# Gated projection with its last two column chunks tile by tile, its split weights in two sets, and a new buffer layout for the second layer's experts

## Chip, cores and metric

One core of one Trainium2 chip runs the whole kernel, one launch. The metric is the device time of one execution in microseconds. The kernel was timed three times; profiled times come from one further execution.

## What is computed

The reference is a trunk of two layers on 1024 positions of width 1024, in float32. Each layer is a token mixer and a mixture of experts, each with its own normalisation. Cut to what the change touches:

```python
def s5_mixer(h, ...):                    # the mixer of layer 1
    ...                                  # state space, y: 1024 x 1024
    y = jax.nn.gelu(y)
    z = y @ w_glu                        # 1024 x 2048: the gated projection
    return z[..., :D] * jax.nn.sigmoid(z[..., D:])

def hierarchical_moe(h, ...):            # behind both mixers
    g_prob = softmax(xt @ w_group + b_group)          # 4 groups, the best one
    e_logits = xt @ w_expert + b_expert               # its 8 experts, the best two
    ...                                               # lists of rows for 32 experts
    hid = silu(xblk @ w_gate[e]) * (xblk @ w_up[e])   # each expert on its rows
    return hid @ w_down[e]

for layer in range(2):
    x = x + g1 * mix(rms_norm(x) * (1 + sc1) + sh1)
    h = rms_norm(x) * (1 + sc2) + sh2
    x = x + g2 * hierarchical_moe(h, ...)
```

## The kernel before

The 1024 positions are eight tiles of 128. A float32 product is made of three products of halves: each operand is split into a high part (a rounding copy) and a low part (a subtraction), and high-high, high-low and low-high are summed in PSUM.

**The gated projection** is the second half of `mixer_b`. Its stationary inputs are `yh[i]` and `yl[i]`, the two parts of the activated tile i. Its weights are taken in four chunks c of 256 columns of each half (value and gate). The loop at L1754 runs over 32 units (chunk, tile): chunk by chunk, and in a chunk tile by tile. A unit is 24 matmuls of 512 columns (L1770), 6 for each quarter q of the contraction. ScalarE's tanh (L1777), a combination on VectorE (L1778) and two operations for the residual update of `x2` (L1780, L1781) follow; the last two are on VectorE for chunk 3 and on GpSimd for the others. `load(c)` brings a chunk of the weights (2 MB) into two buffers of the 16-KB ring; `split(c, q)` makes a quarter's parts `gh` on ScalarE (L1745) and `gl` on VectorE, or GpSimd for half of chunk 0 (L1746). There is one set of `gh` and `gl` of four quarters; the next chunk's are split in the last unit of a chunk. The order of TensorE's work is as written; the other engines follow a scheduler's order.

**The router** (`moe_front`) works beside the projection, in layer 0 beside the attention's output product (L624). Of a unit that is finished, `squares` transposes the columns of the residual (`pt`, L701) and sums their squares on ScalarE, `logits` multiplies them with the router's weights (`lg`, L709) and adds to `lga` (L712). When a tile has all its columns, `scale` finishes the reciprocal root of the mean square with thirteen short operations (L720 to L118) and applies it and the bias to the logits (L723, L724); `rows_in` (L730) and `rows_out` (L736) make the tile's normalised row `hr` and GpSimd stores it to `hrow` in memory (L737). In layer 1, tiles 0 to 5 do so in their groups of three, and two `hr` buffers are in use; in layer 0 there is one, and each tile is scaled by itself. `route` runs for the groups of tiles 0 to 2, 3 to 5 and 6 to 7: VectorE chooses group and experts (L760 to L782, the last being `seen`), TensorE makes prefix sums (`lp`, L786, L787), VectorE makes slots (`so`, L808), and TensorE adds the group to the lists (`lst`, L813). `moe_lists` reads the lists (`lit`, `ligi`, L891, L892). GpSimd then gathers rows by index (`xg`, L956). A tile named `f13hr` is that of layer 1, tile 3; `r10`, `r13` and `r16` are the groups that begin with tile 0, 3 and 6 of layer 1, and `r06` is the last of layer 0.

**The experts** (`moe`): 32 per layer. Gate and up weights of an expert (2 MB) lie in a pair, down weights (1 MB) in a ring buffer x. In both layers experts take turns on two pairs of the ring `w` and two pairs of their own. The SP queue issues all weight loads in program order, each when its buffer is free.

## Time and profile before

| | us |
|---|---|
| median of three runs (lowest, highest) | 1853.67 (1853.0, 1856.04) |
| the profiled execution, its own time | 1852.55 |
| its span, first to last instruction | 1850.6 |
| TensorE busy | 1559.9 (84%) |
| VectorE busy | 1255.6 (68%) |
| ScalarE busy | 748.9 (40%) |
| GpSimd busy | 441.7 (24%) |

The mean granted clock of TensorE is 0.922 of full speed (2.4 GHz). The span is 1.95 us shorter than the execution's own time. Busy shares are means over stages of different kinds: the projection stands at 1220 to 1435 us, the experts of layer 1 behind 1481 us, the end of layer 0's mixer at 500 us.

### The profile page before, as it was taken

To read this page: it belongs to the slowest core of one execution; us is meant where nothing else is said; L and a number is where in the kernel's file an instruction comes from. 1 tells how busy PE (TensorE), PEld (TensorE's weight loads), DVE (VectorE), ACT (ScalarE), POOL (GpSimd) and SP (SyncE) were. 2 spreads that over 40 slices of the span, in tenths; PEclk is the share of its full clock that TensorE was granted. 3 is DMA by queue.
4 is the path that set the end of the run, shared out by engine and by line. 5 is a ranking of instruction groups with operands and counts; after the bars stand their busy time and mean duration, and the time that the engine had idled before them with its cause. 6 is when DMAs were issued, how large, how long until landed. Compare 5 with 4: busy or idle time off the path is not lost. (4 is left out here: it accounts for less than half of the span.)

```text
span 1850.6 us, 20822 instructions
## 1 busy us (share of the span) xinstructions
PE 1559.9 (84%) x6935; PEld 1120.2 (61%) x6935; DVE 1255.6 (68%) x2336; ACT 748.9 (40%) x1455; POOL 441.7 (24%) x385
## 2 busy tenths in 40 slices
PE   5799969899769898899799676769998299999990
PEld 2566623387556666566377565658887277777760
DVE  4886679775578987677355799751226767777764
ACT  3211137611155555455311565532221165656540
POOL 1400014520122121111000677432210212222210
PEclk8799989999879999999899788889999599999995
DMA  9656750062469899887453111421111299999947
GB/s 363 216 211 253 293 153 1 22 220 95 164 230 341 328 328 326 324 312 268 152 208 110 32 36 43 135 76 46 47 46 46 106 389 357 364 382 387 369 149 280
DMA packets 124997, 379.85 MB, mean 205 GB/s; under 512 B 44908, under 2 KB 63428, under 8 KB 94168
## 3 DMA queue, kind: packets, MB, share of 16 engines
q1 hardware_dynamic: 94648, 301.89, 45.2%
q0 software_dynamic: 23040, 50.37, 7.4%
q10 hardware_dynamic: 7200, 26.22, 3.8%
q8 instruction: 57, 0.93, 0.2%
q14 instruction: 52, 0.43, 0.1%
HBM read 355.43 MB, written 56.53 MB: 223 GB/s over the span
## 5 line engine op out<-in xcount | busy, mean ns | idle before, releaser
L1770 PE MATMUL gpo<-gh,yh 128*128 128x512 f32 x256 | 107.1, 418 | 9.8 <-ACT gh L1745 9.8
L1770 PE MATMUL gpo<-gl,yh 128*128 128x512 f32 x256 | 101.7, 397 | 1.7 <-POOL gl L1746 1.7
L1770 PE MATMUL gpo<-gh,yl 128*128 128x512 f32 x256 | 101.6, 397 | 0.0
L956 POOL DMA_INDIRECT xg<-hrow,ligi x64 | 83.6, 1307 | 32.1 <-issue 14.9
L1778 DVE SCALAR_TENSOR_TENSOR gth<-gth,gpo 128x256 f32<-128x256 f32 x32 | 13.4, 420 | 110.4 <-ACT gth L1777 110.4
L222 DVE SCALAR_TENSOR_TENSOR acc<-w,cs,acc 128x2048 f32<-128x2048 f32 x35 | 83.6, 2387 | 4.6 <-DMA w<-in_w_ada 4.1
L1770 PEld LDWEIGHTS gpo<-gh,yh 128*128 128x128 f32 x256 | 49.3, 193 | 18.4 <-ACT gh L1745 10.1
L624 PE MATMUL wopo<-woh,a_hi 128*128 128x512 f32 x128 | 55.4, 433 | 1.7 <-ACT woh L598 1.7
L1770 PEld LDWEIGHTS gpo<-gl,yh 128*128 128x128 f32 x256 | 49.3, 192 | 10.6 <-POOL gl L1746 2.2
L1770 PEld LDWEIGHTS gpo<-gh,yl 128*128 128x128 f32 x256 | 48.9, 191 | 10.6
L624 PE MATMUL wopo<-wol,a_hi 128*128 128x512 f32 x128 | 52.6, 411 | 1.9 <-POOL wol L599 1.9
L1678 PE MATMUL bpo<-wih,bhh 128*128 128x512 f32 x128 | 52.3, 408 | 1.8 <-ACT bhh L1668 1.8
L624 PE MATMUL wopo<-woh,a_lo 128*128 128x512 f32 x128 | 52.6, 411 | 0.0
L1678 PE MATMUL bpo<-wil,bhh 128*128 128x512 f32 x128 | 51.3, 401 | 0.0
L1678 PE MATMUL bpo<-wih,bhl 128*128 128x512 f32 x128 | 50.5, 403 | 0.3 <-DVE bhl L1669 0.2
L1780 POOL TENSOR_TENSOR gth<-gth,g 128x256 f32<-128x256 f32 x24 | 17.5, 729 | 110.0 <-DVE gth L1778 110.0
L1680 DVE SCALAR_TENSOR_TENSOR u<-bpo,n_y,shw 128x512 f32<-128x512 f32 x16 | 12.0, 750 | 29.5 <-PE bpo L1678 29.5
L1678 PEld LDWEIGHTS bpo<-wih,bhh 128*128 128x128 f32 x128 | 24.6, 192 | 9.0 <-ACT bhh L1668 3.7
L624 PEld LDWEIGHTS wopo<-woh,a_hi 128*128 128x128 f32 x128 | 25.5, 200 | 7.2 <-ACT woh L598 2.6
L624 PEld LDWEIGHTS wopo<-wol,a_hi 128*128 128x128 f32 x128 | 25.5, 199 | 7.1 <-POOL wol L599 2.3
L1490 POOL TENSOR_TENSOR s0p<-pw_re,bb 128x512 f32<-128x512 f32 x1 | 1.1, 1082 | 118.4 <-DVE n_y L114 118.4
L1678 PEld LDWEIGHTS bpo<-wih,bhl 128*128 128x128 f32 x128 | 24.4, 191 | 7.5 <-DVE bhl L1669 1.8
(2728 smaller groups left out, 4882.6 us busy)
## 6 DMA issues: line engine op xcount, KB each, us to landing
ring<-in_moe_w_down SPq DMA_DIRECT2D x64, 1024.0 KB
w<-in_w_ada SPq DMA_DIRECT2D x48, 1024.0 KB
w<-in_moe_w_gate SPq DMA_DIRECT2D x32, 1024.0 KB
w<-in_moe_w_up SPq DMA_DIRECT2D x32, 1024.0 KB
pair<-in_moe_w_gate SPq DMA_DIRECT2D x32, 1024.0 KB
pair<-in_moe_w_up SPq DMA_DIRECT2D x32, 1024.0 KB
w<-in_ssm_w_glu SPq DMA_DIRECT2D x16, 512.0 KB
w<-in_attn_w_qkv SPq DMA_DIRECT2D x6, 1024.0 KB
```

Source lines behind the costliest of these rows:

```text
L222: eng.scalar_tensor_tensor(acc, w, self.cs[:, j:j + 1], acc, op0=ALU.mult, op1=ALU.add)
L624: T.matmul(po, a[:, kk, j], w[:, j, :], start=(i == 0), stop=(i == 23))
L956: G.indirect_dma_start(out=self.xg, out_offset=None, in_=me.hrow[l], in_offset=bass.IndirectOffsetOnAxis(ap=self.gcol, axis=0), bounds_che ...
L1490: G.tensor_tensor(self.p1, self.power(me.pw_re, 8), self.channel(me.bb1, 8), op=ALU.mult)
L1678: T.matmul(po, a[:, 4 * hf + j, :], w[:, j, :], start=(k == 0), stop=(k == 23))
L1680: V.scalar_tensor_tensor(u[:, 32 * c:32 * c + 32, 7 - i, :], po.rearrange("p (g c) -> p g c", c=16), r, self.shw[:, 512 * c:512 * c + 512] ...
L1770: T.matmul(po, a[:, 2 * q + j, :], w[:, j, :], start=(n == 0), stop=(n == 23))
L1778: V.scalar_tensor_tensor(th, th, 1.0, po[:, 0], op0=ALU.add, op1=ALU.mult)
L1780: E.tensor_tensor(th, th, g1[:, cs], op=ALU.mult)
```

## The change

**Order of the projection.** `unit_order` puts chunks 0 and 1 chunk by chunk, then for each tile chunk 2 and chunk 3 in a row. Units 0 to 15 are as before, units 16 to 31 are (tile 0, chunk 2), (0, 3), (1, 2) and so on. For layer 0, with two column parts, the order stays.

**Weights.** A quarter has its own load of 512 KB into one of two buffers `graw`, and there are two sets of `gh` and `gl`, for even and odd chunks. The quarters of chunk 1 are split in units 1, 3, 5, 7, those of chunk 2 in units 9, 11, 13, 15, and all of chunk 3 in unit 15.

**Residual update.** It is on VectorE for chunks 2 and 3 of tiles 3 to 7 (10 units), else on GpSimd (22).

**Router, both layers.** The chain of the reciprocal root stands ahead of the last addition of logits; scale and bias are one operation. Each tile is scaled and stored by itself, with one `hr` buffer. In `route`, the rows of the last tile are scaled and stored behind the choice of experts, before gates, slots and lists.

**Buffers.** The ring `w` is closed behind the state space. The experts of layer 1 have four pairs p0 to p3 and three x buffers of their own: p0, x0, p1, x1 where `yl` and `yh` of early tiles lie, p2 and x2 where those of the last tiles and `gl` lie, p3 where the router's tiles lie. Their first loads are issued as p0, x0, p1, x1, p2, x2, p3.

```diff
@@ unit_order
+        return sorted(((m, c) for m in range(NT) for c in range(parts)),
+                      key=lambda u: (u[1], u) if u[1] < parts - 2 else (parts, u))
@@ moe_front
-        gain = fp.tile([P, D], F32, name=f"gain2{l}", tag="hr", bufs=1 + l)
+        gain = fp.tile([P, D], F32, name=f"gain2{l}", tag="hr")
...
+            if c == parts - 1:
+                v = fp.tile([P, 1], F32, name=f"v{l}{m}", tag="v")
+                V.tensor_reduce(v, vs[:, m], AX.X, ALU.add)
+                V.tensor_scalar(v, v, 1.0 / D, EPS, op0=ALU.mult, op1=ALU.add)
+                self.rsqrt(fp, v, [P, 1], "n", r)
             if c:
                 V.tensor_tensor(lg_all[:, m], lg_all[:, m], lg[:, :36], op=ALU.add)
...
+            if c == parts - 1:
+                V.scalar_tensor_tensor(lg_all[:, m], lg_all[:, m], r, br, op0=ALU.mult, op1=ALU.add)
...
+            V.tensor_tensor(ex, mc[:, 1], mc[:, 0], op=ALU.subtract)
+            self.last_exp = S.activation(ex, ex, AF.Exp)
+            if m1 == NT:
+                rows_out(NT - 1)
             V.tensor_scalar(sv["eid"][:, ms, :], mi, -1.0, float(NE), op0=ALU.mult, op1=ALU.add)
             V.tensor_reduce(sg, eg, AX.X, ALU.add)
-            V.tensor_tensor(ex, mc[:, 1], mc[:, 0], op=ALU.subtract)
-            self.last_exp = S.activation(ex, ex, AF.Exp)
...
-                if l == 0 or (c == parts - 1 and m >= GROUPS[-2]):
-                    rows_in(m, width * c, width * c + width)
+                if l == 0 or c >= parts - 2:
+                    rows_in(m, width * c if c > parts - 2 else 0, width * c + width)
...
+            if c == parts - 1 and m + 1 < NT:
+                rows_out(m)
@@ moe
+        if l:
+            weights_in(opened("rga"), "p3")
+            weights_in(opened("rgb"), "p0", "p1", "x0", "x1", "p2")
+            weights_in(opened("rgc"), "x2")
+        else:
+            weights_in(opened("rg", side="right"), "x0", "x1", "x2", "p2", "p3")
...
-                w = self.wpair() if e % GU < N1 else pairs[e % GU - N1]
+                w = pairs[e % GU] if l or e % GU >= N1 else self.wpair()
@@ mixer_b
+            src = wrp.tile([P, 2, 512], F32, name=f"graw{c}{q}", tag="graw", bufs=2)
+            w4 = src.rearrange("p a (h n) -> p a h n", h=2)
+            for h in range(2):
+                self.dma(w4[:, :, h], I["ssm_w_glu"][256 * q:256 * q + 256, 1024 * h + 256 * c:1024 * h + 256 * c + 256]
+                         .rearrange("(a p) n -> p a n", p=P))
+            hi = (wp if c % 2 else wrp).tile([P, 2, 512], F32R, name=f"gh{c}{q}", tag=f"gh{q}")
+            lo = wp.tile([P, 2, 512], F32R, name=f"gl{c}{q}", tag=f"gl{c % 2}{q}")
...
-            for k, (c, i) in enumerate((c, i) for c in range(4) for i in range(NT)):
+            for k, (i, c) in enumerate(self.unit_order(4)):
...
-                    if i == NT - 1 and c < 3:
-                        split(c + 1, q)
+                    if q == 3 and c < 2 and i % 2:
+                        split(c + 1, i // 2)
+                    if (i, c) == (NT - 1, 1):
+                        split(3, q)
...
-                E = V if c == 3 else G
+                E = V if c > 1 and i > 2 else G
```

TensorE before, at the end of the projection (`gpo` is its product; `f17` is the last tile's part of the router):

```order
L1770 MATMUL gpo_11177<-gl_10790,yh_9522 128x512
L1770 MATMUL gpo_11177<-gh_10789,yl_9523 128x512
L786 MATMUL r13lp<-oh_9796,after 128x192
L787 MATMUL r13lp<-seen_9797,ones 128x192
L701 MATMUL f173pt<-ident,x_9683 128x128 x2
L709 MATMUL f163lg<-wr_9770,f163ht 128x128 x2
L813 MATMUL lst_9793<-rv_9799,r13so 128x128 x6
L709 MATMUL f173lg<-wr_9770,f173ht 128x128 x2
L786 MATMUL r16lp<-oh_9796,after 128x128
L787 MATMUL r16lp<-seen_9797,ones 128x128
```

TensorE now, in the last unit but one, where the middle group's prefix product stands:

```order
L1771 MATMUL gpo_11292<-gl_10188,yh_9515 128x512
L1771 MATMUL gpo_11292<-gh_10187,yl_9516 128x512
L715 MATMUL f162lg<-wr_9765,f162ht 128x128 x2
L790 MATMUL r13lp<-oh_9791,after 128x192
L791 MATMUL r13lp<-seen_9792,ones 128x192
L1771 MATMUL gpo_11292<-gh_10276,yh_9515 128x512
L1771 MATMUL gpo_11292<-gl_10277,yh_9515 128x512
```

And now behind the last projection matmul:

```order
L1771 MATMUL gpo_11349<-gh_10482,yl_9516 128x512
L707 MATMUL f173pt<-ident,x_9676 128x128 x2
L715 MATMUL f172lg<-wr_9765,f172ht 128x128 x2
L715 MATMUL f173lg<-wr_9765,f173ht 128x128 x2
L790 MATMUL r16lp<-oh_9791,after 128x128
L791 MATMUL r16lp<-seen_9792,ones 128x128
L892 MATMUL cnt_11517<-seen_9792,ones 128x32
L819 MATMUL lst_9788<-rv_9794,r16so 128x128 x4
```

The middle group's four kinds of product have moved from behind the projection into its last two units, and one group is left behind it.

VectorE before, from the last group's gates to the lists:

```order
L795 TENSOR_TENSOR gatev<-gatev,r16sm 128x2
L797 TENSOR_TENSOR rv_9799<-oh_9796,ids 128x4x32
L800 TENSOR_TENSOR rv_9799<-oh_9796,gatev 128x4x32
L803 TENSOR_TENSOR r16tp<-r16lp,oh_9796 128x128
L804 TENSOR_REDUCE pos<-r16tp 128x4
L808 TENSOR_TENSOR r16so<-slots,pos 128x256 x2
L736 SCALAR_TENSOR_TENSOR f17hr<-f17hr,rms,shr 128x1024
L891 TENSOR_SCALAR lit<-lst_9793 128x32
L892 SCALAR_TENSOR_TENSOR ligi<-lst_9793,lit 128x32
```

VectorE now, from `seen` to the prefix sums of the same group:

```order
L786 TENSOR_TENSOR seen_9792<-seen_9792,oh_9791 128x32 x4
L793 TENSOR_TENSOR r16sm<-r16mc 128x2
L740 SCALAR_TENSOR_TENSOR f17hr<-f17hr,rms,shr 128x1024
L797 TENSOR_SCALAR eid<-r16mi 128x4
L798 TENSOR_REDUCE r16sm<-r16eg 128x2
L799 SCALAR_TENSOR_TENSOR r16sm<-r16sm 128x2
L800 RECIPROCAL gatev<-r16sm 128x2
L801 TENSOR_TENSOR gatev<-gatev,r16sm 128x2
L803 TENSOR_TENSOR rv_9794<-oh_9791,ids 128x4x32
L806 TENSOR_TENSOR rv_9794<-oh_9791,gatev 128x4x32
L809 TENSOR_TENSOR r16tp<-r16lp,oh_9791 128x128
```

The scaling of the last tile's rows has moved from behind the slots to directly behind `seen`.

SP's queue before, the last loads of the projection and the first of layer 1's experts (`pair_0` and `ring_0` are the experts' own buffers, `w` the ring):

```order
L104 DMA w_10449<-in_ssm_w_glu 128x4x256 x4
L104 DMA w_11508<-in_moe_w_gate 128x2048
L104 DMA w_11508<-in_moe_w_up 128x2048
L104 DMA w_11512<-in_moe_w_gate 128x2048
L104 DMA w_11512<-in_moe_w_up 128x2048
L104 DMA w_11537<-in_moe_w_gate 128x2048
L104 DMA ring_0_11465<-in_moe_w_down 128x2048
L104 DMA ring_1_11466<-in_moe_w_down 128x2048
L104 DMA pair_0_11468<-in_moe_w_gate 128x2048
L104 DMA pair_0_11468<-in_moe_w_up 128x2048
```

and now:

```order
L104 DMA graw_10472<-in_ssm_w_glu 128x2x256 x2
L104 DMA graw_10479<-in_ssm_w_glu 128x2x256 x2
L104 DMA pair_p_11561<-in_moe_w_gate 128x2048
L104 DMA pair_p_11561<-in_moe_w_up 128x2048
L104 DMA ring_x_11563<-in_moe_w_down 128x2048
L104 DMA pair_p_11562<-in_moe_w_gate 128x2048
L104 DMA pair_p_11562<-in_moe_w_up 128x2048
L104 DMA ring_x_11564<-in_moe_w_down 128x2048
L104 DMA pair_p_11565<-in_moe_w_gate 128x2048
L104 DMA pair_p_11565<-in_moe_w_up 128x2048
L104 DMA ring_x_11569<-in_moe_w_down 128x2048
L104 DMA pair_p_11557<-in_moe_w_gate 128x2048
```

Down weights have moved ahead of the second and third pair; the pairs are now all the experts' own.

## Rows read from the trace of the kernel before

**Rows 1.** TensorE's waits, 1215 to 1485: releaser, total us, times, longest.

```profile
PE gpo L1770 <- ACT gh L1745: 9.8, 1, 9.8
...
PE r13lp L786 <- DVE eid L789: 6.6, 1, 6.6
```

**Rows 2.** Order of time, TensorE: start, us, operation, idle before.

```profile
1434.75 0.40 PE L1770 MATMUL gpo<-gl,yh 128*128 128x512 f32 x1
1434.98 0.40 PE L1770 MATMUL gpo<-gh,yl 128*128 128x512 f32 x1
...
1450.58 2.96 PE L813 MATMUL lst<-rv,r13so 128*128 128x128 f32 x12 [4.77 <-DVE r13so L808]
...
1481.09 1.97 PE L976 MATMUL e_0pt<-ident,xg 128*128 128x128 f32 x8 [13.87 <-DMA xg<-hrow,ligi]
1482.90 0.79 PE L991 MATMUL e_0gu<-e_0wh,e_0xh 128*128 128x512 f32 x1
```

**Rows 3.** Order of time, end of layer 0's mixer: TensorE, VectorE, GpSimd.

```profile
501.45 0.40 PE L624 MATMUL wopo<-woh,a_lo 128*128 128x512 f32 x1
...
506.91 0.19 DVE L712 TENSOR_TENSOR lga<-lga,f071lg 128x36 f32<-128x36 f32 x1 [1.71 <-PE f071lg L709]
...
519.33 0.53 POOL L737 DMA_DIRECT2D hrow<-f07hr  x1 [4.74 <-DVE f07hr L736]
523.98 1.07 POOL L956 DMA_INDIRECT xg<-hrow,ligi  x1 [4.11 <-DMA hrow<-f07hr]
...
528.44 1.97 PE L976 MATMUL e_0pt<-ident,xg 128*128 128x128 f32 x8 [8.80 <-DMA xg<-hrow,ligi]
```

**Rows 4.** Order of time, VectorE beside the projection.

```profile
1388.52 0.42 DVE L1780 TENSOR_TENSOR gth<-gth,g 128x256 f32<-128x256 f32 x1
...
1406.16 0.95 DVE L730 TENSOR_TENSOR f16hr<-x,scr 128x768 f32<-128x768 f32 x1
```

**Rows 5.** Order of time, VectorE behind the projection, last group.

```profile
1454.43 0.19 DVE L712 TENSOR_TENSOR lga<-lga,f173lg 128x36 f32<-128x36 f32 x1 [2.17 <-PE f173lg L709]
...
1457.50 0.16 DVE L760 TENSOR_REDUCE r16sm<-lga 128x2 f32<-128x8 f32 x1
...
1461.75 0.86 DVE L782 TENSOR_TENSOR seen<-seen,oh 128x32 f32<-128x32 f32 x4
...
1465.35 1.28 DVE L736 SCALAR_TENSOR_TENSOR f17hr<-f17hr,rms,shr 128x1024 f32<-128x1024 f32 x1
1467.26 0.19 DVE L891 TENSOR_SCALAR lit<-lst 128x32 f32<-128x32 f32 x1 [0.64 <-PE lst L813]
```

**Rows 6.** Order of time, GpSimd's queue behind the projection.

```profile
1466.92 0.53 POOL L737 DMA_DIRECT2D hrow<-f17hr  x1 [15.91 <-DVE f17hr L736]
1472.01 3.02 POOL L956 DMA_INDIRECT xg<-hrow,ligi  x1 [4.55 <-DVE rem L914]
```

**Rows 7.** Windows: length, busy time by engine, TensorE clock, DMA share, GB/s.

```profile
522.00:530.00 8.00, 1.56 (x8) 1.56 (x8) 6.02 (x22) 0.40 (x1) 5.06 (x4) 0.50 0.68 252
...
1475.00:1485.00 10.00, 3.91 (x13) 3.25 (x14) 1.42 (x3) 1.19 (x2) 4.01 (x5) 0.50 1.00 387
```

**Rows 8.** Order of time, TensorE at the first group's routing in the projection.

```profile
1412.71 0.98 PE L786 MATMUL r10lp<-oh,after 128*128 128x192 f32 x2 [4.91 <-DVE eid L789]
...
1415.06 0.63 PE L1770 MATMUL gpo<-gl,yh 128*128 128x512 f32 x1
```

**Rows 9.** TensorE's waits, 370 to 530, at layer 0's second routing group.

```profile
PE r03lp L786 <- DVE lga L714: 7.9, 1, 7.9
```

**Rows 10.** VectorE's waits, 400 to 500, with layer 0's one row buffer.

```profile
DVE f06hr L730 <- DMA hrow<-f05hr: 7.1, 1, 7.1
```

**Rows 11.** Order of time, start of the projection: ScalarE, TensorE.

```profile
1220.74 3.90 ACT L1745 ACTIVATE gh<-w 128x1024 fp32r<-128x1024 f32 x4 [4.42 <-DVE yl L1717]
...
1224.34 0.80 PE L1770 MATMUL gpo<-gl,yh 128*128 128x512 f32 x1 [1.71 <-POOL gl L1746]
```

**Rows 12.** Order of time, VectorE at the start of mixer B.

```profile
918.59 1.23 DVE L1658 TENSOR_TENSOR bx<-bx,bya 128x1024 f32<-128x1024 f32 x1 [2.38 <-DMA bya<-yrow]
```

More of the change, by code (lines that the diff above doesn't have):

```diff
@@ L814, in route @@
                              stop=(m == NT - 1 and c == 1))
-        units = [(m, c) for m in range(NT) for c in range(parts)]
-        if l:
-            units.sort(key=lambda u: u[1])
+        units = self.unit_order(parts)
         running, hts, xs, hs = [], {}, {}, {}
@@ L1047, in moe @@
         for e in range(3):
-            load_gate_up(e)
+            if not l or e < 2:
+                load_gate_up(e)
             load_down(e)
+            if l and e == 1:
+                load_gate_up(2)
         load_gate_up(3)
@@ L1747, in split @@
             ws[c, q] = (hi, lo)
-        for c in range(2):
-            load(c)
         for q in range(4):
```

96 lines of the change are left out of this document (34 added, 62 removed).

## The prediction

> **What bounds the kernel now.** The page's busy table makes TensorE the busiest engine, and in both layers' expert loops nothing else can bound it; so I went to TensorE's waits and looked for stretches where it stands still. There are three: the head of the gated projection, the routing inside and behind it, and the stretch from its last matmul to the first expert product. The chain of waits that the page prints ends with the last stores of the program and says nothing on these, so I read the waits of TensorE from 1215 to 1485 us [rows 1], and then the order of time in that stretch [rows 2]. The reader is to see there that the last projection matmul starts at 1434.98 (0.40 us) and that the first expert product starts at 1482.90: **47.5 us**, in which TensorE does little but short router products. What it waits for is one serial chain: two routing groups (tiles 3 to 5 and 6 to 7), VectorE's row scaling, one store, four gathers.
>
> **The tail of layer 1, as it will be.** Three things shorten it. First, group 3 to 5 is routed inside the projection, since tile 5 is complete four units before the end. What is left behind the end is one tile's chain. Layer 0 ends its own projection tile by tile already and gives its lengths: from its last output matmul (501.45 + 0.40) to the last logits addition it takes 5.1 us [rows 3]; layer 1 has one elementwise operation more, 0.42 us [rows 4], and an extra product for column block 2, so I take 6.5. The mean-square chain of thirteen short operations (1454.43 to 1457.50 less three additions: about 2.5 [rows 5]) no longer stands behind the addition but ahead of it, in the time in which VectorE waits for the logits. Second, from the first routing operation to the end of `seen` is 1457.50 to 1461.75 + 0.86 = 5.1 us [rows 5]; with the merged scale-and-bias (0.4) that reaches 12.0 after the end. Third, the last rows are scaled (1.28) right there, not behind the slot products, so their store goes out at about 13.5; before, scaling stood at 1465.35, 2.7 us behind `seen` [rows 5]. The store takes 4.65 us from issue to the gather that waits for it in layer 0 (519.33 to 523.98) and 5.1 in layer 1 (1466.92 to 1472.01) [rows 3, 6]; I take 5.0, so 18.5. The lists came 4.65 behind `seen` (1467.26) [rows 5]; pushed 1.3 us by the scaling, they come at about 18: the two arrive together and the gather starts at 18.6. From gather to first transposition it takes 4.46 us in layer 0 (523.98 to 528.44), but 9.1 in layer 1 (1472.01 to 1481.09) [rows 2, 3, 6]. The difference has its row: in layer 1 the gathers run with the expert weights, at 387 GB/s and DMA share 1.00; in layer 0 at 252 GB/s and 0.68 [rows 7]. After the change four of the seven weight buffers (p0, x0, p1, x1) lie where projection inputs of finished tiles were, and load before the projection ends; p2 and x2 (3 MB) start at its end and at 387 GB/s need about 8 us, long done at 18.6. Only p3 (2 MB), which lies on the router's tiles, starts with the gathers, behind the first one. So I take 4.5: 23.1, plus 1.8 to the first product (1481.09 to 1482.90) = **24.9 against 47.5, -22.6 us.** Bounds: with 9.1 for the gather -18; with the store and gather each 1 us shorter -24.6.
>
> The Trainium skill ("DMA: Bandwidth & Descriptors", Anatomy of one DMA) gives a transfer from the GpSimd queue about 2.0 us and bytes over 436 GB/s; for the 512 KB of a gather that is an estimate of 3.2 us, and the sum would be 1.3 us better. The trace's shortest is 4.46 and I stay with it.
>
> **What moves into the projection.** Group 3 to 5 must now be paid there. Before, its prefix product stood with 6.6 us of waiting [rows 1] and its list products with 4.77 and a duration of 2.96 [rows 2], all behind the end. Inside, TensorE reaches the prefix product at a fixed place in the last unit but one and waits there for VectorE's routing. VectorE then does per tile: two gate operations and four more for the x2 update at 0.42 each (2.5), the rows' first product 0.95 for 768 columns and 0.42 for 256, the scaling 1.28, the mean-square chain 2.5 and some 0.6 of additions [rows 4, 5]: 8.3 us, and a third of a routing group (7.9 for the last one's two tiles, 1457.50 to 1465.35 [rows 5]; I estimate 9.4 for three): about 11.4 of the 12.3 us of two units on TensorE (each 24 matmuls that start 0.23 apart [rows 2], and some 0.6 of router products). It fits, narrowly. A stall of the kind that group 0 to 2 has now (4.91, and then matmuls of 0.63 us rather than 0.40 until TensorE's granted clock is back at 2.4 GHz, some 2 us lost) [rows 2, 8] is what I expect once more: 3 to 5 of waiting, 2 of slow clock, 3.3 of router products that stood behind the end: **+8.3**, bounds +4 (the wait covered) and +14 (as long as the wait of layer 0's second group, which the same one-buffer layout makes 7.9 us [rows 9], with slow matmuls behind it). Group 0 to 2: a stall of 3.9 for 4.9, **-1**, bounds -2 and +3.
>
> **One row buffer in place of two.** Tile i+1's row product must now wait until tile i's rows are stored. Layer 0 works so already: its longest wait there is 7.1 us [rows 10], behind a store issued late after others on GpSimd's queue, which in layer 1 holds only one such store per tile. Scaling ends about 7 us after a tile's last matmul (6.5 as above less the logits, with 1.28), the store lands 5 later, by 12.2, and the next tile's second gate operation can't come before its matmuls end at 12.3 and ScalarE's tanh (0.4) behind them, so the wait lies in time in which VectorE has nothing to do, by half a microsecond. That is a thin cover: if it goes, the price is a rival below. I count **+1** (0 to +4).
>
> **The head of the projection and its weight splits.** Before, TensorE waits 9.8 us for the first split weight and 1.7 for its low part [rows 1, 11]. Now the first two high parts are made while ScalarE is idle, long before; the low parts still need GpSimd and VectorE, which end the previous stage at about 1220, so the second matmul gains about 2. But only two raw buffers exist: the third and fourth quarter are loaded after the first low parts are made, and a 512 KB transfer takes 4.65 us in the nearest row. Third and fourth quarter then come about 2 us later than TensorE wants them. Chunks 1 to 3 are split a quarter at a time, each two units apart (chunk 3 all four in the last unit before the tile-by-tile part, one unit ahead of its use): +1 for those in which a raw buffer is waited for. Together **+2** (-1 to +6). The sum for the projection is +8.3 - 1 + 1 + 2 = **+10.3**.
>
> **Layer 0.** The same moves in the code that both share. The mean-square chain lies in the 1.71 us wait for the last logits [rows 3], so routing starts about 1.5 earlier; merging scale and bias gives 0.2; the rows' store goes out ahead of the lists, near 515.0 in place of 519.33. The gather is then bound by the lists, near 519.7 in place of 523.98: **-4.3** (-2.5 to -5; the low end if the weights' splits on VectorE become the last). Four small side-work loads now stand between expert weights on the SP queue; they are needed some 10 us after they can land: 0.
>
> **Start of mixer B.** SP now issues 1 MB of projection weights, not 4 MB, ahead of the two row loads of which VectorE waits for the first by 2.38 us [rows 12]. That wait goes, and TensorE stood behind VectorE there: **-2.4** (0, if the rows come no earlier, to -2.7).
>
> **Sum.** -22.6 + 10.3 - 4.3 - 2.4 = -19.0. Expert loops, state space and the end of the program: 0, since TensorE works without a gap through the loops before and the loads run as far ahead as they did. The sum stands against the profiled execution, 1852.55 us (span 1850.6), which lies 1.1 below the median of 1853.67; taken from the median it gives 1834.7. The unknown terms of the projection have the longer end upwards, so I write **1835.5**.
>
> **Rivals.**
> *A, the forecast:* 1835.5, own range 1829 to 1842.
> *B, early weights meet the row stores.* p0, p1, x0 and x1 (6 MB) load while the projection runs, in the same microseconds as the rows of tiles 2 to 6 are stored; with one buffer VectorE waits for each of these stores. Priced by the gather (9.1 against 4.46), a store takes 4.6 us more, and two or three of them hit: +9 to +14 less 2 of cover, so about 1845 (1841 to 1851). For it: DMA share 1.00 [rows 7]. Against: each buffer's load is 1 to 2 MB, 3 to 5 us, and falls between stores as easily as on them. The Trainium skill ("Trainium Kernel Development and Optimization", Key Constraints) says the same of the queues: transfers issued from SP, ACT and POOL interleave on the same 16 engines.
> *C, slower:* the split chain. Each quarter's split is load, ScalarE copy, VectorE subtraction, buffer free, next load; a ScalarE copy that waits for its load holds the tanh of the unit behind it, and VectorE's queue holds the next subtraction. If each of the 12 later quarters costs TensorE over 1.6 us net (19 over 12), the change is slower; at half of a 4.65-us transfer, 2.3 each, it is +28 - 19 = +9: 1862. Against: before the last four a quarter has 12.3 us.
> *D, better:* the stall of group 3 to 5 is covered by VectorE running ahead, and the head gains: projection +3, so 1827.
> *E, it doesn't bring what it moves:* the weights' buffers come free only with the lists, gathers stay at 9.1 and the last store stays behind the gathers' other inputs: -22.6 + 4.6 + 4 = -14; the whole -10, 1843.
>
> **How the numbers follow.** A 0.46, B 0.22, C 0.12, D 0.10, E 0.10. About 0.2% (3.7 us) is what a measurement of this kernel can tell from no change, so faster means under 1850.0: A, D, most of B and E: 0.81; within 0.2%: ends of B and C: 0.08; slower: C: 0.11. The range 1826 to 1851 leaves out C and about half of D, 0.17.
>
> **What would show it.** Right: first expert product of layer 1 about 25 us after the last projection matmul, gathers alone on the queues, TensorE waiting once for each of two routing groups inside the projection, and layer 0's first product about 4 us earlier. Wrong: VectorE waits on `hrow` stores over 3 us in layer 1 (B); TensorE waits for `gh` or `gl` behind the first units (C); expert weights loading at the gather (E).

## The result, and the profile after

The changed kernel takes 1839.52 us (median; 1835.48 to 1848.41) against 1855.38 us (1845.46 to 1858.48) for the kernel before on the same chips: **0.9927 times the time before, 95% interval 0.991 to 0.9943**, which is 13.5 us off (the two medians alone lie 15.9 apart). The forecast was 1835.5, from a sum of -19.0. The profiled execution takes 1838.57 us (span 1836.8) against 1852.55 (1850.6), so the two traces differ by 13.8 us of span, which the table lays out; they are called *before* and *after* from here on. A stage ends where the product that is named starts on TensorE, but for "last output product", which is taken at its end (its start in the experiments, where the text says so). Differences are taken before rounding.

| stage | before, us | after, us | difference | forecast |
|---|---|---|---|---|
| start of the program to layer 0's first router transposition (`f000pt`) | 381.2 | 378.8 | -2.4 | 0 |
| to layer 0's last logits product (`f071lg`) | 125.4 | 123.5 | -1.9 | 0 |
| to layer 0's first expert product (`e_0gu`) | 23.6 | 20.2 | **-3.5** | -4.3 |
| to mixer B's first transposition (`bpt`): layer 0's experts, mixer B's first rows | 391.2 | 392.6 | +1.4 | -2.4 |
| to the last state-space product (`s15py`) | 277.6 | 275.8 | -1.8 | 0 |
| to the first router transposition of unit 1 (`f110pt`): head of the projection | 44.9 | 54.1 | **+9.1** | +2 |
| to the last output product of the projection (`gpo`) | 191.3 | 197.9 | **+6.5** | +8.3 |
| to layer 1's first expert product | 47.5 | 24.9 | **-22.7** | -22.6 |
| layer 1's experts, end of the program | 367.7 | 369.1 | +1.5 | 0 |

The first row is code that the change doesn't touch; in the profiled executions of all kernels shown here that stage lasts between 378.8 and 384.8 us, so its -2.4 is no effect. The second (123.4 to 126.0 over the executions of changed code), the fourth (in it the expert loop, 350.7 to 359.0), the fifth (274.7 to 278.0) and the last (367.2 to 369.1 over the executions of changed code but a10) differ likewise by less than what the same code shows from execution to execution. What can be put down to the change lies in four rows: -22.7, -3.5, +9.1, +6.5, together -10.5.

The page's busy table of after (busy us, share of the span, instructions). TensorE has as many instructions as before; what the change moves is when they run.

```profile
PE 1561.8 (85%) x6935; PEld 1121.2 (61%) x6935; DVE 1261.8 (69%) x2390; ACT 750.1 (41%) x1455; POOL 443.7 (24%) x381
```

The waits of TensorE from 1190 to 1480 us of after answer to [rows 1] (engine, tile and line, releaser: total us, times, longest):

```profile
PE gpo L1771 <- POOL gl L1751: 12.2, 2, 10.4
PE gpt L1723 <- ACT gyt L1726: 7.9, 3, 5.3
PE r16lp L790 <- DVE seen L786: 5.9, 1, 5.9
PE e_0pt L986 <- DMA xg<-hrow,ligi: 5.9, 1, 5.9
PE r13lp L790 <- DVE lga L724: 3.3, 1, 3.3
PE r10lp L790 <- DVE lga L724: 2.2, 1, 2.2
```

Group 3 to 5 (`r13lp`) now waits 3.3 us where it waited 6.6, and inside the projection; but the first lines have grown: the wait for a split weight (`gl`) is 10.4 us long, and a new one of 5.3 stands ahead of it, at the transpositions (`gpt`) with which the projection begins.

**The tail of layer 1.** TensorE and GpSimd of after in order of time, with one row of VectorE (start, duration, engine, line, operation, and in brackets the idle time before it and its releaser); this answers to [rows 2, 5, 6]:

```profile
1442.39 0.40 PE L1771 MATMUL gpo<-gh,yl 128*128 128x512 f32 x1
...
1453.72 0.76 PE L790 MATMUL r16lp<-oh,after 128*128 128x128 f32 x2 [5.94 <-DVE seen L786]
...
1465.85 1.97 PE L986 MATMUL e_0pt<-ident,xg 128*128 128x128 f32 x8 [5.91 <-DMA xg<-hrow,ligi]
1467.65 0.79 PE L1001 MATMUL e_0gu<-e_0wh,e_0xh 128*128 128x512 f32 x1
```
```profile
1455.92 0.53 POOL L741 DMA_DIRECT2D hrow<-f17hr  x1 [17.13 <-DVE r16sm L798]
1461.17 1.59 POOL L966 DMA_INDIRECT xg<-hrow,ligi  x1 [4.72 <-DVE blk L900]
```
```profile
1459.98 0.19 DVE L880 TENSOR_SCALAR lit<-lst 128x32 f32<-128x32 f32 x1 [1.83 <-PE lst L819]
```

The last output product ends at 1442.79. From there: store of the last rows at 13.1 us, lists at 17.2, first gather at 18.4, first transposition at 23.1, first expert product at 24.9. The gather takes 4.7 us to the transposition that waits for it (1461.17 to 1465.85), where it took 9.1 [rows 2, 6]. The window around it (length; busy us of TensorE, its weight loads, VectorE, ScalarE and GpSimd with counts; granted clock, DMA share, GB/s) says why, and so does SyncE's queue, with the first loads of the gate weights p0, p2 and p3 (p1's is left out):

```profile
1459.00:1467.00 8.00, 2.09 (x11) 1.80 (x11) 6.88 (x18) 0.40 (x1) 4.91 (x4) 0.50 0.23 60
```
```profile
1365.54 0.34 SPq L104 DMA_DIRECT2D pair_p<-in_moe_w_gate  x1
...
1444.27 0.33 SPq L104 DMA_DIRECT2D pair_p<-in_moe_w_gate  x1
...
1467.91 0.33 SPq L104 DMA_DIRECT2D pair_p<-in_moe_w_gate  x1
```

Between 1459 and 1467 the DMA engines move 60 GB/s at a share of 0.23, where the gather before met 387 GB/s at 1.00 [rows 7]. The early weights load from 1365 on, p2 goes out 1.5 us behind the end of the projection, and p3 only when the first gather is over.

**The end of layer 0.** GpSimd and TensorE of after, which answers to [rows 3]:

```profile
510.37 0.53 POOL L741 DMA_DIRECT2D hrow<-f07hr  x1 [1.01 <-DVE r06sm L798]
515.71 1.55 POOL L966 DMA_INDIRECT xg<-hrow,ligi  x1 [4.80 <-DVE blk L900]
520.65 1.97 PE L986 MATMUL e_0pt<-ident,xg 128*128 128x128 f32 x8 [6.24 <-DMA xg<-hrow,ligi]
```

The last output product there ends at 497.54, so the store goes out at 12.8 us and the gather at 18.2; before they were at 17.5 and 22.1 (519.33 and 523.98 less 501.85 [rows 3]).

**The head of the projection.** First VectorE, TensorE and ScalarE of after, then SyncE's load of the row `g` in after and in before:

```profile
1198.42 0.69 DVE L1755 TENSOR_SCALAR g<-g 128x1024 f32<-128x1024 f32 x1 [9.19 <-DMA g<-ada_d]
```
```profile
1210.18 0.49 PE L1771 MATMUL gpo<-gh,yh 128*128 128x512 f32 x1
1221.12 0.80 PE L1771 MATMUL gpo<-gl,yh 128*128 128x512 f32 x1 [10.45 <-POOL gl L1751]
```
```profile
1224.75 1.06 ACT L1750 ACTIVATE gh<-graw 128x1024 fp32r<-128x1024 f32 x1 [11.35 <-DMA graw<-in_ssm_w_glu]
```
```profile
1191.18 0.32 SPq L104 DMA_DIRECT2D g<-ada_d  x1
```
```profile
1185.09 0.32 SPq L104 DMA_DIRECT2D g<-ada_d  x1
```

In the first row VectorE stands still for 9.19 us for one short operation of 0.69 us, the halving of the gate row `g` (line 1755). Behind it in its queue stand the casts of the transposed mixer output (`yh`), for which TensorE's transpositions and then its products wait. The load of `g` went out at 1191.18, 0.4 us behind the start of the state space's last product (1190.8); before, at 1185.09, it went out 14 us ahead of it (1199.1). In SyncE's order it has moved from ahead of the router's rows (`frows`, `shr`, `scr`) to behind them; only `gain` still follows. So the first cast starts 8.2 us behind that last product's start, against 2.85 before: 5.4 lost. The second loss is inside unit 0: ScalarE's third split waits 11.35 us for a raw buffer to be loaded, and from the second product to the unit's end it takes 10.0 us against 7.1. 5.4 + 2.9 = 8.3 of the 9.1; the rest is about the 0.9 us for which `f110pt` waits for GpSimd's update of `x`. The size of this loss varies: where the head is as in the changed kernel (a4, a6, a7, a10, a12), the traces below have 53.7 to 56.7 us for it, of which unit 0 takes 9.8 to 13.2.

### The profile page after: what moved, and what is told of

Its sections match the earlier page's. It is cut to its first block, busy times and chain, and to the rows that moved or that the text cites. A ratio compares the mean times of both kernels' runs of the same rounds, so it can differ in the third digit from the quotient of the medians.

```text
span 1836.8 us, 20896 instructions
## 1 busy us (share of the span) xinstructions
PE 1561.8 (85%) x6935; PEld 1121.2 (61%) x6935; DVE 1261.8 (69%) x2390; ACT 750.1 (41%) x1455; POOL 443.7 (24%) x381
## 5 line engine op out<-in xcount | busy, mean ns | idle before, releaser
L1691 DVE SCALAR_TENSOR_TENSOR u<-bpo,n_y,shw 128x512 f32<-128x512 f32 x16 | 12.0, 751 | 32.3 <-PE bpo L1689 32.3
L1751 DVE TENSOR_TENSOR gl<-graw,gh 128x1024 fp32r<-128x1024 f32 x14 | 18.5, 1324 | 17.8 <-ACT gh L1750 17.8
```

The source lines that it names most:

```text
L1691: V.scalar_tensor_tensor(u[:, 32 * c:32 * c + 32, 7 - i, :], po.rearrange("p (g c) -> p g c", c=16), r, self.shw[:, 512 * c:512 * c + 512] ...
L1751: (V if c else (G, V)[q % 2]).tensor_tensor(lo, src, hi.bitcast(F32), op=ALU.subtract)
```

## The experiments

Theory 1: the tail's gain is the moved group of tiles and a gather that has the DMA engines to itself; the head's loss is VectorE's queue blocked by `g`, and two raw buffers for four quarters. Theory 2, the rival: the tail's gain is the store ahead of the lists, and the projection loses because VectorE has too much to do (splits and the update of x2). "Head" is from the last `s15py` to `f110pt` (before 44.9, after 54.1), "tail" from the start of the last `gpo` to that of the last product of expert 0's first group, `e_0gu` (before 55.3, after 32.7). Ratios are to the kernel before on the same chip, with 95% intervals. The expectations speak of 5.6 and 25.6 us for the changed kernel's gather and first product; the rows above give 4.7 and 24.9.

### a1: the row `g` loaded early

```diff
-        g1 = self.row(gp, 1, 2, "g1")
+        g1 = self.row(wrp, 1, 2, "g1")
```

> The changed kernel with one edit: the row g1 lies in the pool of the raw weights, whose space is free long before, so that its load is issued early and not behind the router's rows. Theory 1 (the head of the projection lost its time because VectorE stood 9.2 us at the halving of g1, waiting for that load, with the splitting of the activations queued behind it): that wait is gone, the second projection matmul starts 5 us earlier relative to the first transposition of the state space's output (30.2 us after it in the changed kernel, 25 expected), and the whole is 5 us faster than the changed kernel. Theory 2 (the head is bound by the activations on ScalarE and GpSimd's share of the low parts, and VectorE's wait only uses up slack): the interval stays at 29 to 30 us and the whole within 1 us.

1843.75 us, 0.9942 [0.9921, 0.9964]; head 54.4. No gain over the changed kernel's 0.9927, but it is no test of the theory either, as VectorE's row shows:

```profile
1206.78 1.22 DVE L664 SCALAR_TENSOR_TENSOR scr<-scr,gain 128x1024 f32<-128x1024 f32 x1 [9.25 <-DMA gain<-in_norm_ffn]
```

The wait for `g` is gone, and the next short operation on a loaded row, the router's scale (line 664), now stands at the queue's head in its place, for 9.25 us instead of 9.19. The scheduler had put the one where the other was.

### a3: the same, and four raw buffers for the first chunk

```diff
-            src = wrp.tile([P, 2, 512], F32, name=f"graw{c}{q}", tag="graw", bufs=2)
+            if c == 0 and q > 1:
+                src = wp.tile([P, 2, 512], F32, name=f"graw{c}{q}", tag=f"gl1{q}")
+            else:
+                src = wrp.tile([P, 2, 512], F32, name=f"graw{c}{q}", tag="graw", bufs=2)
```

> As a1_g_early, and the raw third and fourth quarter of chunk 0 have buffers of their own (tiles that are used only later), so that their loads wait for no subtraction. Theory 1 (two raw buffers make TensorE wait inside unit 0: 9.9 us from the second matmul to the end of the unit, 7.0 before the change): the unit takes 7 us again, and the whole is 3 us faster than a1_g_early, 8 faster than the changed kernel, about 1831. Theory 2 (TensorE would wait for the low parts on VectorE and GpSimd anyway, since both are late): 0 to 1 us against a1_g_early.

1834.97 us, 0.9909 [0.9878, 0.9939]; head 50.6, 3.8 less than in a1 where 3 was expected. Unit 0 is shorter (8.3 us from second product to end, 10.1 in a1 and 10.0 in after), and so is `f110pt`'s wait behind it; the wait ahead of unit 0 has not gone. So the raw buffers cost 3.8 us of the head's loss.

### a8: both short operations put behind the splits of the mixer's output

```diff
-        V.scalar_tensor_tensor(scr, scr, 1.0, gain, op0=ALU.add, op1=ALU.mult)
+        if l:
+            with self.tc.issue_after(self.last_yl.ins):
+                V.scalar_tensor_tensor(scr, scr, 1.0, gain, op0=ALU.add, op1=ALU.mult)
...
-        V.tensor_scalar(g1, g1, 0.5, None, op0=ALU.mult)
+        with tc.issue_after(self.last_yl.ins):
+            V.tensor_scalar(g1, g1, 0.5, None, op0=ALU.mult)
```

(`last_yl` is the last subtraction that makes a low part `yl`.)

> The changed kernel with one edit: on VectorE the halving of g1 and the combination of scr with the gain stand behind the last splitting of the activations (a1_g_early had only exchanged one for the other at the head of the queue). Theory 1 (VectorE's wait of 9 us at a row load, with the splitting queued behind it, is the larger part of what the head of the projection lost): no such wait, and from the last state-space product to the transposition of unit 1 about 49 us, 5 less than the 54.1 of the changed kernel (44.9 before the change). Theory 2 (the loads merely fill time that GpSimd's and ScalarE's shares of the same stage take anyway): 53 to 54 us.

1833.5 us, 0.9871 [0.9846, 0.9895]; head 48.7, against 49 expected and 54.1 in after. VectorE's first cast and TensorE's waits:

```profile
1197.46 0.43 DVE L1731 CAST yh<-gyt 128x512 fp32r<-128x512 f32 x1 [4.46 <-ACT gyt L1730]
```
```profile
PE gpo L1776 <- POOL gl L1755: 10.6, 2, 8.8
...
PE gpt L1727 <- ACT gyt L1730: 3.6, 5, 1.6
```

VectorE now waits only for ScalarE's copy of the transposition, not for a load, and TensorE's wait at `gpt` falls from 7.9 to 3.6 us. That is 5.4 us against after for the order of two short operations (5.0 to 8.0 against the other traces with the changed head): the part that theory 1 gave to the blocked queue.

### a9 and a11: a8 with the raw buffers of a3

> a8_after_yl and a3_both's buffers for the raw third and fourth quarter of chunk 0. Theory 1 (the two losses of the head are separate, 5.5 us at the row loads and 3.8 us at the two raw buffers): 45 to 46 us from the last state-space product to the transposition of unit 1, as before the change, and 8 to 9 us faster than the changed kernel: about 1831. Theory 2 (the two overlap: with VectorE early, the first quarters' low parts come early too and the raw buffers free in time): no more than 1 to 2 us better than a8_after_yl.

1832.79 us, 0.9866 [0.9842, 0.989]; head 44.1, where 45 to 46 was expected: 4.6 less than in a8, somewhat more than the 3.8 that the same buffers gave in a3, and near before's 44.9 again. The whole time shows little of it (0.9866 against a8's 0.9871, far inside their intervals); the raw buffers' part is read from the head alone. What is left of TensorE's waits there:

```profile
PE gpo L1779 <- POOL gl L1758: 8.8, 1, 8.8
```

The second short wait for `gl` is gone; the long one stands where before waited 9.8 us for `gh` [rows 1]. This version beats both kernels, so it ran once more on one chip with the changed kernel:

> a9_both once more, beside the changed kernel on the same chip. If the 9 to 10 us that its head is shorter are worth that in the time of the whole, it is 8 to 10 us (0.5%) below a12_changed_again; if the expert loops or the routing give part of it back, 3 to 5 us.

> The changed kernel itself, beside a11_a9_again on the same chip: a ratio to before of 0.991 to 0.994 is expected by both theories; from the last state-space product to the transposition of unit 1 54 us.

a11: 1830.17 us (1828.17 to 1833.9), 0.9887 [0.9869, 0.9905]. a12, the changed kernel: 1838.9 us, 0.9936 [0.9917, 0.9955]. The intervals don't overlap; 8.7 us, in the 8 to 10 expected. The heads are 44.1 and 56.0; for the second, 54 was expected.

### a7: the last rows behind the lists, all else as changed

```diff
             self.last_exp = S.activation(ex, ex, AF.Exp)
-            if m1 == NT:
-                rows_out(NT - 1)
...
                     pass
+                rows_out(NT - 1)
```

> The changed kernel with one part undone: in both layers the last tile's rows are scaled and stored behind the lists' products and not ahead of the gates. Theory 1 (the store is on the path, about 5 us from its issue to the gather): the gather starts some 4 us later in each layer, the whole is 7 to 8 us slower than the changed kernel. Theory 2 (the lists set the gather's start, and the store has slack): 0 to 2 us.

1847.2 us, 0.9962 [0.9942, 0.9981]. Layer 1's tail is 32.3 us, against 32.7 with the rows ahead: nothing. GpSimd in layer 1:

```profile
1471.74 0.53 POOL L741 DMA_DIRECT2D hrow<-f17hr  x1 [20.53 <-DVE f17hr L740]
1475.60 1.73 POOL L965 DMA_INDIRECT xg<-hrow,ligi  x1 [3.33 <-DVE rem L902]
```

The projection ends at 1456.7 in this trace, so the store goes out at 15.0 us (13.1 in after), the lists are there at 15.4 (17.2), and the gather starts at 18.9 (18.4). What the rows gain by going first, the lists lose by VectorE's scaling ahead of them. In layer 0 the same edit costs 7.4 us (27.6 from `f071lg` to `e_0gu`, 20.2 in after):

```profile
517.92 0.53 POOL L741 DMA_DIRECT2D hrow<-f07hr  x1 [3.92 <-DVE f07hr L740]
522.60 3.50 POOL L965 DMA_INDIRECT xg<-hrow,ligi  x1 [4.14 <-DVE e_0wl L975]
```
```profile
532.93 1.97 PE L985 MATMUL e_0pt<-ident,xg 128*128 128x128 f32 x8 [14.71 <-DMA xg<-hrow,ligi]
```
```profile
527.00:531.00 4.00, 0.00 (x0) 0.00 (x0) 0.00 (x0) 0.00 (x0) 2.42 (x3) 0.50 1.01 406
```

Here the gather takes 10.3 us (522.60 to 532.93; 4.9 in after). The next expert weights go out at 523.84, 1.2 us behind it, and the queues then run at 406 GB/s. So 5.4 of the 7.4 us are the longer gather and the rest its later start: in layer 0 the order of rows and lists pays mostly by what it spares the gather. Weights beside it are not the whole reason: at the end of layer 0 before, they go out 1.3 us behind the gather too, and it takes 4.46 us [rows 3]. There its issue held GpSimd for 1.07 us, here for 3.50; how much of the 10.3 is due to each stays open. The whole, 6.5 us over the changed kernel by the ratios, is near theory 1's 7 to 8, but not by its mechanism in layer 1.

### b1: the kernel before with the last rows ahead of gates and lists

```diff
             self.last_exp = S.activation(ex, ex, AF.Exp)
+            if m1 == NT:
+                rows_out(NT - 1)
...
                     pass
-                rows_out(NT - 1)
```

> The kernel before, with one part of the change alone: in both layers the last tile's rows are scaled and stored ahead of the gates and lists. Theory 1 (what a7_rows_last lost in layer 0, 7.3 us, was the store's place alone): layer 0's last logits product to first expert product 3 to 4 us shorter than the 23.6 of before (the lists then set the gather), layer 1 2 to 4 us; the whole 5 to 8 us faster than before. Theory 2 (in layer 0 the 7.3 us came from the gather's meeting with the next 2 MB of weights, which the store's place only triggers): layer 0 gains 1 to 4 us, layer 1, whose gathers run with the weights either way, 0 to 1.

1852.03 us, 0.9965 [0.9947, 0.9984]. The first expert product comes 1.6 us earlier in layer 0, and 5.8 in layer 1, whose tail is 6.3 us shorter (49.0 against 55.3). GpSimd, TensorE and SyncE there:

```profile
1469.84 1.59 POOL L957 DMA_INDIRECT xg<-hrow,ligi  x1 [4.73 <-DVE blk L912]
```
```profile
1474.82 1.97 PE L977 MATMUL e_0pt<-ident,xg 128*128 128x128 f32 x8 [6.21 <-DMA xg<-hrow,ligi]
```
```profile
1474.26 0.33 SPq L104 DMA_DIRECT2D w<-in_moe_w_gate  x1
```

The gather takes 5.0 us, not 9.1: the next weights go out 4.4 us behind its start, where they went out 0.8 behind. But from the last `e_0gu` of expert 0's first group to the same product of expert 31 it then takes 317.9 us against 313.1: 4.9 of the 6.3 are given back, since those weights are late (ScalarE's split for expert 2 waits 6.2 us for its second half). Neither theory has this right: layer 0 came out as theory 2 said, layer 1 gained more than either, and the whole, 6.5 us by the ratio, lies in theory 1's 5 to 8, while the profiled execution is no shorter than before's (span 1850.9 against 1850.6). What the store's place alone is worth in the whole is thus between nothing and 6.5 us. Of the tail's 22.7 us it explains 6.3 at most, and in the new layout nothing (a7): theory 2 falls for the larger part of the tail.

### a10: the changed kernel with all of layer 1's weights behind the lists

```diff
             blocks[e].gather()
+        if l:
+            with tc.issue_after(self.routed.ins):
+                for t in [pairs[k] for k in range(GU)] + ring2:
+                    V.memset(t[:, 0:1], 0.0)
+                    V.memset(t[:, 2047:2048], 0.0)
+                for k in range(GU):
+                    V.memset(pairs[k][:, 2048:2049], 0.0)
```

> The changed kernel with one edit: a column of each of layer 1's weight buffers is set by VectorE behind the lists, so that all of its first weight loads start only then, beside the gathers (the edit of a4_weights_late moved only the loads of p2, x2 and p3; the scheduler kept p0, x0, p1 and x1 early). Theory 1 (early weights are what keeps the gather short): gather to first transposition about 9 us in place of 5.6, and the first product some 8 us later than in the changed kernel, since the 2 MB of its weights (5.4 us at 387 GB/s and the start of a transfer) and their split follow the lists. Theory 2 (gather and weights don't disturb each other): gather to transposition 5 to 6 us; only the weights' own arrival delays the first product, by 3 to 6 us.

1850.39 us, 0.9965 [0.9943, 0.9987]: about half of the change's gain is gone. SyncE, GpSimd and TensorE:

```profile
1454.01 0.34 SPq L104 DMA_DIRECT2D pair_p<-in_moe_w_gate  x1
```
```profile
1454.18 1.06 POOL L966 DMA_INDIRECT xg<-hrow,ligi  x1 [4.72 <-DVE pair_p L1059]
```
```profile
1462.20 1.97 PE L986 MATMUL e_0pt<-ident,xg 128*128 128x128 f32 x8 [9.25 <-DMA xg<-hrow,ligi]
```

With the weights going out in the same microsecond, the gather takes 8.0 us, near before's 9.1 and theory 1's 9; from 1456 to 1462 the DMA engines move 410 GB/s. The first product comes 29.4 us behind the projection's end (1436.4), 4.5 later than in after, within theory 2's 3 to 6 and not theory 1's 8. The tail is 6.0 longer (38.6 for 32.7), and another 3.9 is lost among the experts (317.3 us from expert 0 to expert 31, measured as in b1; 313.4 in after). So the early buffers of the new layout carry a good part of the tail's gain, at the first product and behind it. They have a price, too: without them the projection takes 192.1 us, not 197.9 (196.1 to 199.4 in all other traces of changed code), little more than before's 191.3; the section on the prediction shows where.

### a4: p3's load moved ahead in the code

```diff
             blocks[e].gather()
+        if l:
+            load_gate_up(3)
...
-        load_gate_up(3)
+        if not l:
+            load_gate_up(3)
```

> The changed kernel with one edit: in layer 1 the pair p3, whose space is free only when the router is done, is loaded first, so that all other expert weights wait behind it in SP's queue and load while the rows are gathered, as before the change. Theory 1 (the early weights are what makes the gather short, 5.6 us from its issue to the first transposition against 9.1 before): the gather takes about 9 and the first product besides waits for its weights (3 MB at 387 GB/s, 8 us, then a split of 1 to 2), so that first product comes 35 us or more behind the last projection matmul, not 25.6; the whole is 8 to 12 us slower than the changed kernel. Theory 2 (the order of the router's work alone brings the gain, and gather and weights don't disturb each other): within 3 us of the changed kernel.

1844.05 us, 0.994 [0.992, 0.996]. The edit did not do what it was made for: p0, x0, p1 and x1 still load early, and only the rest of p2, x2 and p3 moved (p2's up half to 1471.88, behind the gather). The tail is 31.6, the gather 4.9. It says only that late p2 and x2 cost little (expert 0 to 31 in 314.6 us, 313.4 in after); a10 took its question up.

### a6: all updates of x2 on GpSimd

```diff
-                E = V if c > 1 and i > 2 else G
+                E = G
```

> The changed kernel with one part altered: all residual updates behind the projection are on GpSimd, none on VectorE (10 units fewer there, two operations of 0.42 us each). Theory 1 (TensorE's two stalls at the routing inside the projection, 2.8 and 3.5 us, come from VectorE's load beside the routing operations): each stall is 1 us or more shorter, since one or two updates of 0.85 us stand between the routing's operations in VectorE's queue; behind the projection the update is 0.6 us longer (0.73 for 0.42, twice). The whole 1 to 2 us faster or the same. Theory 2 (the stalls come from the chain of routing operations itself and the wait for the one row buffer): the stalls stay within 0.5 us, and the whole is 0 to 1 us slower.

1843.0 us, 0.995 [0.9933, 0.9968]. TensorE's waits:

```profile
PE r13lp L790 <- DVE lga L724: 3.7, 1, 3.7
PE r10lp L790 <- DVE lga L724: 3.0, 1, 3.0
```

With less on VectorE the routing stalls are not shorter (3.3 and 2.2 in after). The edit changed more than VectorE's load: an update on GpSimd takes 0.73 us and not 0.42, so tile 5's last logits come later (VectorE waits 0.9 us for them). The plainer test is a10. VectorE is as busy in its projection as in that of after (82.6 and 82.7 us), and the stall of group 3 to 5 is 0.7 us: it does not come from VectorE's load, and the second half of theory 2 falls too.

## Why the prediction was right where it was, and wrong at the head

**The tail of layer 1 was right term by term.** Forecast, from the end of the projection: store 13.5, lists 18, gather 18.6, transposition 23.1, product 24.9. Measured: 13.1, 17.2, 18.4, 23.1, 24.9. The gather's 4.4 us are shown by experiment: it is short when weights don't run beside it (4.7 in after, 5.0 in b1, 8.0 in a10), and the early buffers are what keeps them away (a10). The larger piece, the last store going out 13.1 us behind the projection and not 31.5, is read from the traces: the middle group's waits and list products on TensorE, 14.3 us together (6.6, 4.77 and 2.96 [rows 1, 2]), stood behind the end before and now stand inside. That they make most of these 18.4 us is argued; no run moves that group alone. The third step needs a correction. I gave "the last rows are scaled right there" a share of the gain; a7 shows that in layer 1 it is worth nothing by itself, since the lists are pushed by as much as the store is pulled. In layer 0, where early buffers aren't what parts the two, it is worth 7.4.

The Trainium skill ("DMA: Bandwidth & Descriptors", Anatomy of one DMA) would have made the gather an estimate of 3.2 us. The trace doesn't agree: 4.7 here, 4.46 at the end of layer 0 before [rows 3]. The other rule cited from the Trainium skill, that transfers of different queues interleave on the same 16 engines ("Trainium Kernel Development and Optimization", Key Constraints), agrees with a10's 8.0 us beside weight loads.

**What moved into the projection was a little less than forecast,** +6.5 for +8.3, but not for the reason given. Group 3 to 5 stalls for 3.5 us where 3 to 5 was said. My working put that down to VectorE's own work, 11.4 of 12.3 us, and put the wait for the one row buffer into "time in which VectorE has nothing to do". The rows of after, VectorE and TensorE, show that wait in the middle of the group's routing (L769 and L770 are two steps of it):

```profile
1419.42 0.16 DVE L769 TENSOR_REDUCE r13sm<-r13t 128x3 f32<-128x12 f32 x1
1422.16 0.96 DVE L734 TENSOR_TENSOR f16hr<-x,scr 128x768 f32<-128x768 f32 x1 [2.58 <-DMA hrow<-f15hr]
1423.03 0.16 DVE L770 TENSOR_TENSOR r13t<-desc,r13sm 128x12 f32<-128x12 f32 x1
...
1427.68 1.00 PE L790 MATMUL r13lp<-oh,after 128*128 128x192 f32 x2 [3.34 <-DVE lga L724]
```

The store of tile 5's rows went out at 1416.57, beside a load of expert weights, and VectorE could go on 5.6 us later. In a10, where no expert weights load in the projection, the same store goes out at 1413.82, and neither VectorE nor TensorE waits much:

```profile
1416.75 0.95 DVE L734 TENSOR_TENSOR f16hr<-x,scr 128x768 f32<-128x768 f32 x1
...
1422.27 0.59 PE L790 MATMUL r13lp<-oh,after 128*128 128x192 f32 x2 [0.69 <-DVE lga L724]
```

The windows around the store in after and in a10, and the one behind the stall in after:

```profile
1416.00:1422.00 6.00, 6.00 (x31) 4.98 (x30) 2.81 (x12) 1.49 (x5) 0.53 (x1) 1.00 0.81 311
```
```profile
1413.00:1419.00 6.00, 6.00 (x31) 4.98 (x30) 5.06 (x19) 1.49 (x5) 0.53 (x1) 1.00 0.22 87
```
```profile
1428.00:1434.00 6.00, 5.76 (x21) 4.43 (x21) 5.32 (x27) 0.44 (x2) 0.00 (x0) 0.74 0.01 4
```

The store meets 311 GB/s at a DMA share of 0.81 in after and 87 at 0.22 in a10; behind the stall TensorE's granted clock is 0.74 in after, and in a10 it stays at 1.00. In every trace with the changed kernel's placement of the updates, the stall is VectorE's wait for this store and 0.7 to 0.8 us more (1.9 and 2.7 in a3, 2.6 and 3.3 in after, none and 0.7 in a10). Group 0 to 2 follows the same rule with the store of tile 2: a wait of 1.4 and a stall of 2.2 in after, 0.8 and 1.6 in a10. So 5.8 of the 6.5 us go with the early weights, through the single row buffer, a term that I had at +1. That the stall came out within my 3 to 5 is luck. Group 0 to 2 now stalls 2.2 + 0.6 us where it stalled 4.9: -2.1, and I had -1. Two row buffers with the early weights were not tried.

**The head is the step that failed:** "together +2 (-1 to +6)", and +9.1 was measured. Its working priced the splits of the weights, and there it was partly right: raw buffers that come late were seen, as "about 2 us", and cost 3.8 to 4.6 (a3 against a1, a9 against a8). What it left out is VectorE's queue. The new layout moved `g`'s load behind the router's rows, and one operation of 0.69 us at the head of VectorE's queue held everything behind it for 9.2. That costs 5.4 us (a8), and with both repaired the head is 44.1, 0.9 under before: that is all that the early high parts have left on balance, where I had counted a gain of about 2. The prediction counted the moved loads of the weights and not that of this row.

**Layer 0:** -3.5 for -4.3, with the mechanism as written. The store goes out at 12.8 us (forecast 515.0 - 501.85 = 13.2), the gather at 18.2 (17.9). Layer 0's experts show +1.4 behind it, but that loop varies by 8 us between executions, so nothing is read from this.

**Mixer B was wrong in kind:** -2.4 forecast, a gain of 0.2 to 0.4 measured (the wait for the first row is 0.4 shorter, the two waits together 0.2). "That wait goes" - it didn't. VectorE and ScalarE's queue, to be read beside [rows 12]:

```profile
911.93 1.23 DVE L1669 TENSOR_TENSOR bx<-bx,bya 128x1024 f32<-128x1024 f32 x1 [1.96 <-DMA bya<-yrow]
913.76 1.23 DVE L1670 TENSOR_TENSOR bx<-bx,byb 128x1024 f32<-128x1024 f32 x1 [0.60 <-DMA byb<-yrow]
```
```profile
905.35 0.33 ACTq L1667 DMA_DIRECT2D bya<-yrow  x1
```

From issue to use the first row takes 6.6 us where it took 7.0, although SyncE issued 1 MB and not 4 MB ahead of it. The step put the wait down to the amount of weights ahead, and a quarter of them is enough to keep it: in those 6.6 us the DMA engines still move 308 GB/s at a share of 0.92 (358 at 1.04 before). How much of the time is the row's own no run shows.

**The sum.** Against the forecast, layer 0 is off by +0.8, the head by +7.1, the projection by -1.8, and mixer B by +2.0 to +2.2: -19.0 becomes about -10.8, as the four stages and mixer B say. The trace has -13.8. The missing 3 us lie in the stages put down to variation (-2.4, -1.9, -1.8, +1.5, and the rest of the fourth, +1.6 to +1.8); what of them belongs to the change after all stays open. The ratio gives -13.5, with -10.6 to -16.7 as its interval. So the measured time is near the forecast partly by luck: -10.8 would have been within its range, but not as near.

**The rivals.** *A* is what came, by its time and its tail; the head and mixer B missed, and the row buffer's term was mis-sized. *B*: waits for row stores were to exceed 3 us; the longest is 2.6. By that sign B is out, but its mechanism, early weights that meet row stores, is there, at 5.8 us where B had 7 to 12. *C*: TensorE was to wait for splits behind the first units; its only such wait there is 0.8 us. Its mechanism, the chain of load, copy and subtraction, did come true in unit 0, where a quarter has no 12 us. *D*: the stall of group 3 to 5 is not covered. *E*: no weights load at the gather, since the layout frees the buffers early.

## What to carry to other kernels

A gather on the critical path was priced here by what else the DMA engines carried in those microseconds, and weights that are there already kept it short. But loading them early has a price where they meet other short transfers: here they saved 9.9 us in the tail and the experts (a10) and cost 5.8 in the projection, where a row store stood on the path through a single buffer. So follow each early load to the time at which it now runs, and ask which wait lies there. When a change moves a load of any size within a queue, look up which short operation waits for it and what stands behind that on its engine: an operation of 0.7 us held an engine for 9.2. And an edit that removes such a wait is to be read in the trace before it is believed, for the scheduler may fill the place with the next one, as in a1; putting an order on the operation (a8) removed it.

## What the runs showed of the hardware

The time of one gather of rows by index, from its issue on GpSimd to the transposition that waits for it, is 4.7 to 5.3 us in the traces where the next weights go out 3 us or more behind it, and 8.0 to 10.3 beside expert weights at 387 to 410 GB/s (before, a7, a10). The end of layer 0 before stands apart: weights go out 1.3 us behind the gather, 252 GB/s, and it takes 4.46 us [rows 3, 7]. The issue itself took between 1.06 and 3.50 us on GpSimd for the same instruction (a10 and a7). A store of 512 KB of rows held its buffer for 5.6 us beside 311 GB/s (after) and for 2.9 at most beside 87 (a10). And code that no edit touched differs by some microseconds between executions: the first 380 us of the program ended between 378.8 and 384.8, layer 0's expert loop from expert 0 to 31 took 350.7 to 359.0. With intervals of some 0.2% either way, whole times of kernels 0.3% apart hardly decide on a single edit; the stages do.
